# A hybrid decoder layer on one core: a second buffer for the prompt rows of the compression, value products given out later, and identity transposes at the start

## The chip, the cores and the metric

The kernel runs on one core of a Trainium2 chip. The metric is the device time of one execution in microseconds (us); lower is better. The core has TensorE (PE in the profile, with PEld for its weight loads), VectorE (DVE), ScalarE (ACT), GpSimd (POOL) and SyncE (SP). DMA transfers are issued from SP's and POOL's queues, each of which works in its own order: an issue that has to wait holds up all issues behind it on that queue.

## The reference, cut to what matters

One layer of a decoder trunk is computed for 512 prompt tokens and for 32 sample tokens (8 samples of 4), which share all weights; the model width is 2048 and everything is float32. After an RMSNorm one input projection (2048 by 7712) gives the queries, keys, values, gates and forget values of two groups of eight heads of 128:

```
z = einsum('btd,dc->btc', h, w_in)
out = einsum('bnchd,cde->bnhe', blk + pe, w)            # compress: 32 rows to one, for keys and for values
o = g[0] * o_compressed + g[1] * o_selected + g[2] * o_window      # the nsa group
s = q.k * scale + dq - dk ; o = softmax(s).v                       # the fox group, D = cumsum(log f)
y = x + einsum('btc,cd->btd', concat(o_n * silu(z_n), o_f * silu(z_f)), w_out)
```

For the samples the keys and values of 1024 earlier tokens lie in pages of 128 rows that a page table names, for both groups, and the nsa group has a window buffer of 512 rows besides. New keys and values go out as results; a final RMSNorm closes the trunk. The nsa group's compressed keys and values come from the cache's rows for the samples and from the new rows for the prompt.

## The kernel before, in words

**Tiles of the input projection.** The projection is cut into tiles of 128 output columns (`run_tiles`). A tile takes four loads of weights (`raw`, 256 KB each). `w_split` makes of each a high part on ACT (`whi`) and a low part on DVE (`wlo`), and PE adds the three products of high and low parts (`mm3`) in the PSUM tiles `pz`; so a quarter of a tile is 24 products of 128 by 272. Five `raw` buffers and three `whi`/`wlo` buffers let the loads and splits run ahead: the split is written two quarters before its products, and the load of a later quarter is written behind the `wlo` that frees its buffer. Quarters are numbered m; tile 0 (gates and forget values) has a path of its own in float32 (`w`), and the quarters 4, 5, ... belong to tiles 1, 2, .... Afterwards a tile's result `zt` goes to its `post` function, which for keys and values transposes it on DVE (`nat`) and writes it out (`store_natural`).

**What orders the work.** Everything else is written as Python generators, "streams": `start` (normalisation and transposition of x), `compress`, `nsa_prompt`, `nsa_sample`, `fox_sample`, `fox_prompt` and others. While the kernel is built, a model of the engines (`Clock`) keeps a time for each engine and for the DMA queues. Between products of the projection `S.pump()` lets each stream go on that is due by this clock. A stream that yields a list of tiles goes on once the model takes these tiles for ready; `S.after(us)` lets it go on once the model's PE is `us` further; a string waits for a flag. The result is a fixed order on each engine; on the chip only semaphores hold instructions back. So the pieces of the streams stand between the products of the projection, and a wrong guess of the model becomes a wait at the head of an engine's queue.

**The places of the change.** The compression's generator `compress` first takes the prompt's rows, which the tiles "c00 c01" (keys) and "c10 c11" (values) have just written to the result `nsa_kv_prompt`: for each of the two it waits for the flags, loads the rows back into the tile `cz` with eight DMAs of 16 by 8 by 128, yields `[cz]` and `S.after(8.0)`, and transposes them on DVE into `more0` or `more1`. There is one `cz` buffer, so the loads for the values wait for the transposition for the keys. Then 64 steps with gathered cache rows (`crow`, transposed into `ct`, split into `cxh`/`cxl`) and weights (`cw`) follow.

`fox_sample` is run twice, for four heads each. Its last part multiplies the probabilities `pt` (`fpt` in the profile) with pages of values `fpg`: two query groups `bq` of four steps `kp`, each with two pages of 256 KB. There are two page buffers, and the next two pages' loads are written behind the products (`ahead`), half of them on SP and half on POOL. The products go to the PSUM tile `accv`. `nsa_sample` has a similar end for each of two groups of samples: six steps of two sets of rows `spg` (five buffers), products in `acc`; the same five buffers carry the sets for its scores, which DVE transposes into `skt`.

`start` loads x in four quarters of 512 columns (`xt`, the first in two halves) and transposes each with 16 PE transposes (`pre`), from which ACT makes `h_hi` and DVE `h_lo`. Before x arrives it gives 16 transposes of the identity (`tr<-ident`) to PE, and 17 small ones of the norm's weights and of the samples.

Of the kernel before, what the change touches and what calls it, by code (L numbers as in the profile page):

```python
# [8 lines left out]
F32 = mybir.dt.float32  # L9
# [6 lines left out]
P = 128  # L16
# [283 lines left out]
def dram(ap, offset, dims):  # L300
    return bass.AP(tensor=ap.tensor, offset=ap.offset + offset, ap=dims)
# [3 lines left out]
def trunk_step(ctx, tc, x_prompt, x_sample, cache_nsa_kv, cache_fox_kv, cache_fox_logf, state_nsa_win,  # L305
# [4 lines left out]
    nc = Engines(tc.nc, clock)  # L310
# [20 lines left out]
    S = Streams(clock)  # L331
# [44 lines left out]
    def tr_tile(shape, name="tr"):  # L376
        return psum.tile(shape, F32, name=name, tag="tr", bufs=2)
# [4 lines left out]
    def cp(out, in_, scale=1.0):  # L382
        nc.scalar.activation(out, in_, AF.Copy, scale=scale)
# [19 lines left out]
    def mm(out, a, b, start=True, stop=True):  # L403
        nc.tensor.matmul(out, a, b, start=start, stop=stop, skip_group_check=True)
# [8 lines left out]
    ident = cst.tile([P, P], F32, name="ident")  # L413
# [457 lines left out]
    def load(t, src):  # L871
        nc.sync.dma_start(t, src)
        return t
# [210 lines left out]
    def fox_sample(hh):  # L1084
# [119 lines left out]
        for bq in range(2):  # L1204
            acc = psum.tile([P, SEQ], F32, name="accv", tag="accv", bufs=1)
            for kp in range(4):
                pgs = [pages.pop(at[1] + x) for x in range(2)]
                yield [*pgs, pt, acc]
                for x in range(2):
                    kb = kp * 2 + x  # L1210
                    for b in range(4):
                        o = kb * P + (bq * 4 + b) * 16
                        mm(acc[b * 32:b * 32 + 32], pt[:, o:o + 32], pgs[x][:, b], kb == 0, kb == 7)
                at[1] += 2
                yield
                ahead()
            ob = obs[bq]
            cp(ob, acc)
            yield
            yield from S.take()  # L1220
            tp = tr_tile([P, 4, P])
            for g in range(4):
                nc.tensor.transpose(tp[:, g, :], ob[:, g * P:(g + 1) * P], ident)
            yield
            for g in range(4):
                nc.vector.tensor_copy(o_s[:, 8 + hh * 4 + g, bq * 16:bq * 16 + 16].rearrange("p (b t) -> p b t", t=4),
                                      tp[:, g, :].rearrange("p (b r) -> p b r", r=32)[:, :, g * 4:g * 4 + 4])
            S.put()
# [17 lines left out]
    def compress(pl):  # L1246
# [17 lines left out]
        def load_w(s):  # L1264
            if s < 32:
                cg, kv, dp = s // 4, s // 2 % 2, s % 2
                cw[s] = t = pl.tile([P, 2, P], F32, name="cw", bufs=3)
                for d in range(2):
                    load(t[:, d], dram(cmp_w, (kv * 32 + cg * 4) * P * P + (dp * 2 + d) * 32 * P, [[P * P, 4], [P, 32], [1, P]]))
        load_rows(0)  # L1270
        load_w(0)
        load_w(1)
        more = []
        for kv in range(2):
            yield (f"nkv{kv}0", f"nkv{kv}1")
            yield [dram(nsa_kv_prompt, kv * 256 + v * P, [[1024, SEQ], [1, P]]) for v in range(2)]
            cz = pl.tile([P, 8, P], F32, name="cz")
            for c in range(4):
                for v in range(2):
                    load(cz[c * 32 + v * 16:c * 32 + v * 16 + 16],  # L1280
                         dram(nsa_kv_prompt, kv * 256 + v * P + c * 1024, [[32 * 1024, 16], [4 * 1024, 8], [1, P]]))
            yield [cz]
            yield S.after(8.0)
            m = pl.tile([P, 32, MORE], F32, name=f"more{kv}")
            more.append(m)
            nc.vector.memset(m[:, :, 33:], 0.0)
            nc.vector.tensor_copy(m.rearrange("p (g d) k -> p g d k", d=4)[:, :, :, 32],
                                  peT[:, :, kv * 8:kv * 8 + 8].rearrange("p d g -> p g d"))
            nc.vector.transpose(m[:, :, :32], cz.rearrange("p g d -> p (g d)"))
            yield  # L1290
# [12 lines left out]
        for step in steps + [None]:  # L1303
            if step:
                cg, bh, kv, dp = step
# [6 lines left out]
                n = 256 if bh else WIDE  # L1312
# [19 lines left out]
        for kv in range(2):  # L1332
            bc = pl.tile([P, 1], F32, name="bc", bufs=2)
            nc.vector.tensor_copy(bc, pss[kv][:, 288:289])
            pc = pl.tile([P, 32], F32, name="pc", bufs=2)
            nc.vector.tensor_scalar(pc, pss[kv][:, 256:288], bc, None, op0=OP.add)
            vt = pl.tile([P, 2, 8, 32], F32, name="vt", bufs=2)
            for bh in range(2):
                src = (psb[:, kv] if bh else pss[kv][:, :256]).rearrange("p (b v n) -> p v b n", b=4, v=2)
                for v in range(2):  # L1340
                    nc.scalar.activation(vt[:, v, bh * 4:bh * 4 + 4], src[:, v], AF.Identity, bias=bc)
            yield
            vf = vt.rearrange("p v b n -> p v (b n)")
            if kv == 0:
                nc.sync.dma_start(kp_scr, pc)
                nc.sync.dma_start(kc_scr, vf)
            else:
                yield from S.take(2)
                tp = tr_tile([P, 2, 256])
                for grp in range(2):  # L1350
                    for v in range(2):
                        nc.tensor.transpose(tp[:, grp, v * P:(v + 1) * P], vf[:, v, grp * P:(grp + 1) * P], ident)
                tq = tr_tile([16, 2, P])
                for v in range(2):
                    nc.tensor.transpose(tq[:, v, :], pc[:, v * 16:(v + 1) * 16], ident)
                yield
                vn = pl.tile([P, 2, 256], F32, name="crow", bufs=2)
                cp(vn, tp)
                vq = pl.tile([P, 2, P], F32, name="cw", bufs=3)[:16]
                cp(vq, tq)  # L1360
                S.put(2)
                yield
                nc.sync.dma_start(vc_scr, vn)
                nc.sync.dma_start(vp_scr, vq)
# [188 lines left out]
    def nsa_sample(pl):  # L1553
# [82 lines left out]
        for grp in range(2):  # L1636
# [14 lines left out]
            for x in range(2):  # L1651
                a, b = slice(64 * x, 64 * x + 64), slice(64 - 64 * x, 128 - 64 * x)
# [66 lines left out]
            for br in range(2):  # L1719
# [34 lines left out]
                p = T("sp", [P, 1024 + 64]) if br == 0 else p  # L1754
# [51 lines left out]
            def values(k, srcs, n=P, first=False, last=False):  # L1806
                for bb in range(4):
                    mm(acc[bb * 32:bb * 32 + 32], PT[:n, k, bb * 32:bb * 32 + 32], srcs[bb], first, last)
            yield [acc, PT]
            for k in range(0, 12, 2):  # L1810
                ts = [got.pop(0) for _ in range(2)]
                yield ts + [vc] * (k == 8)
                if k == 8:
                    values(12, [vs] * 4, 64)
                    values(13, [vc[:, grp, :]] * 4)
                for x in range(2):
                    values(k + x, [ts[x][:, bb] for bb in range(4)], first=k + x == 0, last=k + x == 11)
                yield ts
                set_in()
                set_in()  # L1820
# [82 lines left out]
    def add_in(col, post):  # L1903
# [4 lines left out]
                 n=lambda h, _: add_in(C_QN + h * P, post_qn(h)),  # L1908
                 q=lambda h, _: add_in(C_QF + h * P, post_qf(h)),
                 k=lambda h, _: add_in(C_KF + h * P, post_kf(h)),  # L1910
                 v=lambda h, _: add_in(C_VF + h * P, post_vf(h)),
# [6 lines left out]
    def start():  # L1918
        with tile_pool("pre") as pre:
# [27 lines left out]
            ts = tr_tile([P, KT, 32], "pres")  # L1947
            for k in range(KT):
                nc.tensor.transpose(ts[:, k, :], xs[:, k * P:(k + 1) * P], ident[:32, :32])
            for k in range(KT):  # L1950
                c = k // 4
                if k % 4 == 0:
                    yield [xt[:, c]]
                tag, bufs = (("s", 2), ("accv", 1), ("s", 2), ("acc", 1))[k % 4]
                tp = psum.tile([P, SEQ], F32, name="pre", tag=tag, bufs=bufs)
                yield [tp]
                for i in range(4):
                    nc.tensor.transpose(tp[:, i * P:(i + 1) * P], xt[:, c, i, (k % 4) * P:(k % 4 + 1) * P], ident)
                g = gT[:, k:k + 1]
                nc.scalar.activation(h_hi[:, k, :SEQ], tp, AF.Copy, scale=g)  # L1960
                nc.vector.scalar_tensor_tensor(h_lo[:, k, :SEQ], tp, g, h_hi[:, k, :SEQ], op0=OP.mult, op1=OP.subtract)
                flags.add(f"x{k}")
                if k == 3:
                    flags.add("begun")
                    hs = pre.tile([P, KT, 32], F32, name="hs")
                    nc.vector.tensor_tensor(hs, ts, gT[:, :, None].to_broadcast([P, KT, 32]), op=OP.mult)
                    cp(h_hi[:, :, SEQ:], hs)
                    low(h_hi[:, :, SEQ:], h_lo[:, :, SEQ:], hs)
# [186 lines left out]
```

## Time and profile before

| what | value |
|---|---|
| time, median of 3 runs | 1295.4 us (1294.78 to 1297.54) |
| time of the profiled execution | 1292.8 us, of which the span of the profile is 1291.1 us |
| PE busy | 1254.9 us, 97% of the span |
| DVE, ACT, POOL busy | 784.5, 549.8, 284.5 us |
| share of the chain that ended last | PE 73%, DMA 10%, "issue" 9% |
| input projection with all streams | from 16.8 to 1082.7 us |
| output projection | from 1082.7 us to the end |
| DMA | 266.86 MB, 207 GB/s in the mean |

The span is cut into slices on the profile's page, and a row of it shows the busy share of each engine. An engine's row in a timeline is its start, its duration, the engine, the operation with the tiles written and read, the number of merged instructions and, in square brackets, the idle time before it and what ended it. In the table of waits a row names who waited for whom, the sum in us, the number of times and the longest. A table of windows gives the busy time of each engine in a stretch, with the number of instructions in brackets, then the granted share of the PE clock, the DMA share and GB/s.

### The profile page before, as it was taken

How to read it: one execution, taken by the hardware profiler on the slowest of the kernel's cores; microseconds unless marked ns; L12 is line 12 of the kernel's file. 1: busy time of each engine (PE TensorE's matmuls, PEld its weight loads, DVE VectorE, ACT ScalarE, POOL GpSimd, SP SyncE). 2: the span in 40 equal slices, each digit the busy share in tenths (PEclk: the TensorE clock that was granted, in tenths of full speed). 3: DMA queues.
4: the chain of work that ended last, by engine and by line, in shares of the span. 5: the costliest groups of instructions: out<-in, count | busy, mean ns of one | idle time of the engine just before them, and what ended most of it. 6: DMA issues, size and time to landing. Idle time of an engine off the chain costs nothing.

```text
span 1291.1 us, 27195 instructions
## 1 busy us (share of the span) xinstructions
PE 1254.9 (97%) x10071; PEld 1130.4 (88%) x10071; DVE 784.5 (61%) x1978; ACT 549.8 (43%) x1193; POOL 284.5 (22%) x376
## 2 busy tenths in 40 slices
PE   8989999999999999999999999899999999999997
PEld 6989999998789999999998888688889988777786
DVE  6735888885546667655687753386566537354255
ACT  5313333434334677652345452256754524333221
POOL 5221277753410000005445012211111200000000
PEclk9989999999999999999999999999999999999999
DMA  7476699998986455659967688977788697334323
GB/s 214 129 192 170 178 279 298 299 288 272 295 272 160 121 157 155 174 157 292 294 199 235 174 239 244 257 211 198 217 233 202 196 304 258 100 114 147 127 76 139
DMA packets 308398, 266.86 MB, mean 207 GB/s; under 512 B 87198, under 2 KB 255150, under 8 KB 307592
## 3 DMA queue, kind: packets, MB, share of 16 engines
q1 hardware_dynamic: 284312, 189.15, 51.4%
q0 software_dynamic: 23904, 75.84, 18.3%
q8 instruction: 79, 1.29, 0.4%
q14 instruction: 55, 0.45, 0.1%
q10 hardware_dynamic: 48, 0.13, 0.0%
HBM read 236.32 MB, written 37.05 MB: 212 GB/s over the span
## 4 chain that ended last, share of the span: by engine, by line
PE 73%; DMA 10%; issue 9%; POOL 2%; DVE 2%; SPq 2%; ACT 2%; POOLq 0%; DVEq 0%; ACTq 0%
PE pz L169 40%; PE po L169 15%; DMA fpg<-in_cache_fox_kv 4%; PE tr L169 4%; PE accv L169 4%; PE s L169 4%; PE acc L169 3%; SPq L169 2%; DMA spg<-in_cache_nsa_kv 1%; POOL crow L169 1%; PE psb L169 1%; DMA spg<-in_state_nsa_win 1%; PE accf L169 1%; DMA xt<-in_x_prompt 1%; POOL fpg L169 1%
## 5 line engine op out<-in xcount | busy, mean ns | idle before, releaser
L169 PE MATMUL pz<-h_hi,whi 128*128 128x272 f32 x1920 | 565.6, 295 | 2.2 <-DVE zt L169 1.6
L169 PE MATMUL pz<-h_hi,wlo 128*128 128x272 f32 x1920 | 554.9, 289 | 5.8 <-DVE wlo L169 5.8
L169 PE MATMUL pz<-h_lo,whi 128*128 128x272 f32 x1920 | 554.4, 289 | 0.0
L169 PEld LDWEIGHTS pz<-h_hi,whi 128*128 128x128 f32 x1920 | 363.4, 189 | 18.2 <-issue 13.6
L169 PEld LDWEIGHTS pz<-h_hi,wlo 128*128 128x128 f32 x1920 | 362.8, 189 | 6.0 <-DVE wlo L169 6.0
L169 PEld LDWEIGHTS pz<-h_lo,whi 128*128 128x128 f32 x1920 | 363.3, 189 | 0.8
L169 DVE TENSOR_TENSOR wlo<-raw,whi 128x512 fp32r<-128x512 f32 x275 | 186.0, 678 | 157.7 <-ACT whi L169 152.9
L169 ACT ACTIVATE whi<-raw 128x512 fp32r<-128x512 f32 x275 | 171.5, 625 | 210.4 <-PE pz L169 96.9
L169 POOL DMA_INDIRECT fpg<-in_cache_fox_kv,fi x128 | 131.6, 1028 | 300.4 <-ACT whi L169 209.7
L169 PE MATMUL po<-whi,h_hi 128*128 128x512 f32 (+1 forms) x256 | 95.5, 373 | 0.0
L169 POOL DMA_INDIRECT crow<-in_cache_nsa_kv,ci x64 | 66.0, 1031 | 125.6 <-DVE ct L169 71.8
L169 PE MATMUL po<-whi,h_lo 128*128 128x512 f32 (+1 forms) x256 | 93.4, 365 | 0.0
L169 PE MATMUL po<-wlo,h_hi 128*128 128x512 f32 (+1 forms) x256 | 93.4, 365 | 0.0
L169 DVE STREAM_TRANSPOSE ft<-fpg 128x1024 f32<-128x1024 f32 x64 | 78.9, 1235 | 17.3 <-DMA fpg<-in_cache_fox_kv,fi 13.2
L169 ACT ACTIVATE cxh<-ct 128x580 fp32r<-128x580 f32 (+1 forms) x64 | 42.2, 660 | 85.1 <-DVE ct L169 75.2
L169 DVE TENSOR_TENSOR zt<-pz,rsb 128x272 f32<-128x272 f32 x56 | 24.6, 439 | 85.3 <-PE pz L169 85.3
L169 POOL DMA_DIRECT2D spg<-in_cache_nsa_kv x64 | 35.0, 546 | 185.3 <-DVE skt L169 57.6
L169 ACT ACTIVATE zt<-pz 128x272 f32<-128x272 f32 x66 | 26.2, 398 | 98.7 <-PE pz L169 98.5
L169 PEld LDWEIGHTS po<-whi,h_hi 128*128 128x128 f32 x256 | 48.1, 188 | 19.7 <-ACT whi L169 7.5
L169 POOL DMA_DIRECT2D fpg<-in_cache_fox_kv x64 | 34.8, 544 | 133.8 <-PE accv L169 96.0
L169 DVE TENSOR_TENSOR cxl<-ct,cxh 128x580 fp32r<-128x580 f32 (+1 forms) x64 | 46.1, 720 | 19.4 <-ACT cxh L169 18.6
L169 PEld LDWEIGHTS po<-whi,h_lo 128*128 128x128 f32 x256 | 48.2, 188 | 8.5
(409 smaller groups left out, 1907.1 us busy)
## 6 DMA issues: line engine op xcount, KB each, us to landing
raw<-in_w_in SPq DMA_DIRECT2D x240, 256.0 KB
fpg<-in_cache_fox_kv POOLq DMA_DIRECT2D x64, 256.0 KB, 7.0
fpg<-in_cache_fox_kv SPq DMA_DIRECT2D x64, 256.0 KB
raw<-in_w_out SPq DMA_DIRECT2D x40, 256.0 KB
spg<-in_cache_nsa_kv POOLq DMA_DIRECT2D x64, 128.0 KB, 5.4
spg<-in_cache_nsa_kv SPq DMA_DIRECT2D x64, 128.0 KB
out<-in_state_nsa_win SPq DMA_DIRECT2D x32, 254.0 KB
scr_z<-zt SPq DMA_DIRECT2D x28, 272.0 KB
```

What stands on the lines that cost most here:

```text
L169: return fn(*a, **k)
```

## The change

The change has four edits.

1. In `compress` the loads of the prompt's rows for the keys and for the values are written in a first loop, into two `cz` buffers, and both transpositions in a second loop behind it, each with its own `[cz]` and `S.after(8.0)`. The small tile `vt` at the end of `compress` becomes a part of a `cz` buffer, so that the memory stays the same.
2. In `fox_sample` every step of the value products waits a further `S.after(1.5)` once its pages are due.
3. In `nsa_sample` every step of the value products does the same.
4. In `start` a function `keep_on` gives 14 transposes of the identity to PE, into a PSUM tile that nobody reads. It is called before the first quarter's transposes and again behind them.

```diff
@@ fox_sample
             for kp in range(4):
                 pgs = [pages.pop(at[1] + x) for x in range(2)]
                 yield [*pgs, pt, acc]
+                yield S.after(1.5)
                 for x in range(2):
@@ compress
-        more = []
+        more, czs = [], []
         for kv in range(2):
             yield (f"nkv{kv}0", f"nkv{kv}1")
             yield [dram(nsa_kv_prompt, kv * 256 + v * P, [[1024, SEQ], [1, P]]) for v in range(2)]
-            cz = pl.tile([P, 8, P], F32, name="cz")
+            czs.append(pl.tile([P, 8, P], F32, name="cz", bufs=2))
             for c in range(4):
                 for v in range(2):
-                    load(cz[c * 32 + v * 16:c * 32 + v * 16 + 16],
+                    load(czs[kv][c * 32 + v * 16:c * 32 + v * 16 + 16],
                          dram(nsa_kv_prompt, kv * 256 + v * P + c * 1024, [[32 * 1024, 16], [4 * 1024, 8], [1, P]]))
+        for kv, cz in enumerate(czs):
             yield [cz]
             yield S.after(8.0)
             m = pl.tile([P, 32, MORE], F32, name=f"more{kv}")
...
-            vt = pl.tile([P, 2, 8, 32], F32, name="vt", bufs=2)
+            vt = pl.tile([P, 8, P], F32, name="cz", bufs=2)[:, :4].rearrange("p (v b) (c n) -> p v (b c) n", v=2, n=32)
@@ nsa_sample
                 ts = [got.pop(0) for _ in range(2)]
                 yield ts + [vc] * (k == 8)
+                yield S.after(1.5)
                 if k == 8:
@@ start
             for k in range(KT):
                 nc.tensor.transpose(ts[:, k, :], xs[:, k * P:(k + 1) * P], ident[:32, :32])
+            idle = tr_tile([P, 4, P])
+
+            def keep_on():
+                for k in range(14):
+                    nc.tensor.transpose(idle[:, k % 4, :], ident, ident)
+            keep_on()
             for k in range(KT):
...
                 if k == 3:
+                    keep_on()
                     flags.add("begun")
```

Since the planner's clock sees all four edits, it places the streams' pieces anew from there on. Three places show this. In what follows `-` is the kernel before and `+` the changed one.

PE's order at the start (`tr<-ident` are the identity's transposes, `pre` those of x, `pres` those of the samples):

```order
-L169 MATMUL pre<-ident,xt 128x128 x32
+L169 MATMUL tr<-ident 128x128 x14
+L169 MATMUL pre<-ident,xt 128x128 x16
+L169 MATMUL tr<-ident 128x128 x14
+L169 MATMUL pre<-ident,xt 128x128 x16
```

Fourteen transposes stand ahead of the first quarter of x, and fourteen between the first and the second.

DVE's order where the compression's prompt rows are transposed (`more`, from `cz`), between the splits of weights for m = 16, 17 and later:

```order
 L169 TENSOR_TENSOR wlo<-raw,whi 128x512
 L169 TENSOR_TENSOR zt<-pz,rsb 128x272
-L169 MEMSET more_993 128x32
-L169 COPY more_993<-peT 128x32
-L169 STREAM_TRANSPOSE more_993<-cz 128x32x32
-L169 TENSOR_TENSOR wlo<-raw,whi 128x512
-L169 TENSOR_TENSOR zt<-zt,rsb 128x272
+L169 TENSOR_TENSOR wlo<-raw,whi 128x512
+L169 TENSOR_TENSOR zt<-pz,rsb 128x272
 L169 STREAM_TRANSPOSE nat<-zt 128x544
 L169 TENSOR_TENSOR wlo<-raw,whi 128x512 x3
```

The first transposition no longer stands ahead of the split for m = 17; in the changed kernel it comes ten splits later, behind that for m = 26, and the second one three splits behind it.

SP's order behind the loads of `cz` and the writes `scr_f` of that time:

```order
 L169 DMA scr_f<-ft 4x32x128 x4
-L169 DMA raw<-in_w_in 128x4x128 x2
-L169 DMA out<-nat 4x32x32
-L169 DMA out<-nat 32x16x32 x4
+L169 DMA raw<-in_w_in 128x4x128
+L169 DMA out<-nat 4x32x32
+L169 DMA out<-nat 32x16x32 x2
+L169 DMA raw<-in_w_in 128x4x128
+L169 DMA out<-nat 32x16x32 x2
 L169 DMA raw<-in_w_in 128x4x128 x3
```

Three writes of results now stand ahead of the load of weights for m = 22.

## The prediction

> **What bounds the kernel now.** I read the page first, then PE's waits, then the windows around the longest of them.
>
> ```profile
> span 1291.1 us, 27195 instructions
> PE 1254.9 (97%) x10071; PEld 1130.4 (88%) x10071; DVE 784.5 (61%) x1978; ACT 549.8 (43%) x1193; POOL 284.5 (22%) x376
> ```
>
> PE is busy for 97% of the span and no other engine for more than 61%. So PE's order is the path: a microsecond counts if PE stands still in it or runs at less than its full clock, and 1291.1 − 1254.9 = 36 us is all the standing still there is. The table of PE's waits names most of it:
>
> ```profile
> PE pz L169 <- DVE wlo L169: 5.8, 1, 5.8
> PE accv L169 <- DMA fpg<-in_cache_fox_kv: 5.2, 6, 1.5
> PE pre L169 <- DMA xt<-in_x_prompt: 2.4, 2, 1.3
> PE acc L169 <- DMA spg<-in_state_nsa_win: 2.1, 1, 2.1
> PE pz L169 <- DVE zt L169: 1.6, 1, 1.6
> PE accf L169 <- DVE fptl L169: 1.6, 1, 1.6
> PE tr L169 <- DVE scr L169: 1.5, 1, 1.5
> ```
>
> The change aims at the first four rows, 15.5 us together. The rest are single short waits that a new order may lengthen or shorten.
>
> **Edit 1, the compression's prompt rows.** The timelines of DVE and PE show where the 5.8 us come from:
>
> ```profile
> 79.68 1.25 DVE L169 STREAM_TRANSPOSE more<-cz 128x1024 f32<-128x1024 f32 x1 [8.10 <-DMA cz<-out]
> 80.85 0.65 DVE L169 TENSOR_TENSOR wlo<-raw,whi 128x512 fp32r<-128x512 f32 x1
> 81.55 0.60 PE L169 MATMUL pz<-h_hi,wlo 128*128 128x272 f32 x1 [5.80 <-DVE wlo L169]
> ```
>
> DVE waits 8.1 us at the head of its queue for the rows in `cz`; behind it stands the low part of the weights of m = 17, and PE waits for that. In the changed order this split comes first and the transposition ten splits later. At the pace of the splits (ACT rows below, one each 3.0 us) that is 30 us, and 8.1 are needed, so the wait goes whole: −5.8. After the wait PE is slow for a while:
>
> ```profile
> 81.50:85.20 3.70, 3.65 (x16) 3.65 (x17) 2.27 (x4) 0.00 (x0) 0.00 (x0) 0.51 0.83 270
> 85.20:92.00 6.80, 6.80 (x56) 6.80 (x56) 1.73 (x3) 1.27 (x2) 0.00 (x0) 1.00 0.74 174
> ```
>
> At a granted clock of 0.51 sixteen products take 3.7 us; at 1.00 56 take 6.8, 0.121 each, and sixteen 1.9. Without the standstill this stretch has its clock, −1.8. What is late next is the supply of weights, for SP is full just then:
>
> ```profile
> 68.82 5.75 SPq L169 DMA_DIRECT2D cz<-out  x8
> 74.67 0.53 SPq L169 DMA_DIRECT2D raw<-in_w_in  x1
> 75.71 3.57 SPq L169 DMA_DIRECT2D scr_f<-ft  x4
> 79.38 2.52 SPq L169 DMA_DIRECT2D raw<-in_w_in  x2
> 82.66 4.18 SPq L169 DMA_DIRECT2D out<-nat  x5
> ...
> 89.12 0.63 ACT L169 ACTIVATE whi<-raw 128x512 fp32r<-128x512 f32 x1 [2.38 <-PE pz L169]
> 92.13 0.63 ACT L169 ACTIVATE whi<-raw 128x512 fp32r<-128x512 f32 x1 [2.37 <-PE pz L169]
> ...
> 872.83 5.21 DMA raw<-in_w_in
> ```
>
> The load at 74.67 is that of m = 20; those of 21 and 22 follow at 79.38. In the changed order three of the five `nat` writes (0.84 us each by the row) get ahead of m = 22, so it goes out at about 79.4 + 1.3 + 2.5 = 83.2. With 5.2 us for a load (the last row, from the chain of waits) it lands at 88.4, and `whi` and `wlo` (0.63 and 0.65) make it ready at about 89.8. PE stops at 81.55 − 5.80 = 75.75, a few products into m = 17, which began at 75.4; no longer held, it would begin m = 22 five quarters of 3.0 us later, at 90.4. That is cover by 0.6 us only. For m = 21 (out at 79.4, ready at 86.0, due at 87.4) it is 1.4. If a load took 7.6 us, as the page load at 820.51 below, m = 22 would be 1.8 late; I take 0.4 between 0 and 1.8. The compression itself begins later, by two waits of 8 us on the planned clock instead of one after the second load; products of the projection fill that. Edit 1: −5.8 − 1.8 + 0.4 = −7.2, bounds −7.6 and −5.8.
>
> **Edits 2 and 3, the value products.** The 5.2 us of the second wait fall into the two runs of `fox_sample` (the same table, cut at 296 to 385 and at 740 to 832 us):
>
> ```profile
> PE accv L169 <- DMA fpg<-in_cache_fox_kv: 2.3, 3, 0.8
> PE accv L169 <- DMA fpg<-in_cache_fox_kv: 2.9, 3, 1.5
> ```
>
> None is over 1.5 us, so products that stand 1.5 us further back find their pages, if the pages come when they come now. They don't quite: the next pages are loaded into the buffers that these products free, so each load moves as well, by 1.5 us for each step before it; but the interval between one step's products and the next step's grows by the same 1.5, and the wait is set by this interval alone. In the chain of waits the steps and loads read so:
>
> ```profile
> 763.84 1.85 PE accv L169 x16
> 774.32 1.85 PE accv L169 x16
> ...
> 800.66 9.94 DMA fpg<-in_cache_fox_kv
> ...
> 820.51 7.61 DMA fpg<-in_cache_fox_kv
> ```
>
> Steps are 10.5 us apart and a load takes up to 9.9 after its issue. For the first run I take −2.1 of 2.3. In the second run the changed order puts more of the samples' sets `spg` among the pages: on POOL's queue 14 set loads stand among the last 16 page loads, where there were two. So I take −1.0 of 2.9. The single wait in `nsa_sample` was 2.1 us; 1.5 of it is covered, −1.5. It too is followed by a stretch at half clock:
>
> ```profile
> 945.30:948.70 3.40, 1.32 (x14) 0.64 (x13) 1.17 (x4) 2.45 (x5) 2.20 (x4) 1.00 1.13 279
> 948.70:952.20 3.50, 3.45 (x20) 2.64 (x20) 0.43 (x2) 1.21 (x4) 0.71 (x2) 0.51 1.09 266
> ```
>
> At 0.51 instead of 1.00 3.5 us hold 1.7 of loss. Whether the clock falls depends on how idle PE is in the 3.4 us before (1.32 busy here), so I count −1.2. The delays lengthen the streams by 16 × 1.5 = 24 us (fox) and 12 × 1.5 = 18 us (nsa), which costs only what the projection can't cover; the chain has this cover:
>
> ```profile
> 1051.11 31.57 PE pz L169 x252
> ```
>
> After the last step of `nsa_sample` 31.6 us of products of the projection remain, and in the changed order there are more of them behind it (339 products of `pz` behind the last `acc`, 261 before, counted in the two orders). Cost 0; without that cover it would be up to 18. Edits 2 and 3: −2.1 − 1.0 − 1.5 − 1.2 = −5.8; bounds 0 and −(5.2 + 2.1 + 1.7) = −9.0.
>
> **Edit 4, the transposes at the start.**
>
> ```profile
> 1.52 3.68 PE L169 MATMUL tr<-ident 128*128 128x128 f32 x16 [1.52 <-DVE ident L169]
> 5.26 1.91 PE L169 MATMUL pres<-ident,xs 32*128 32x32 f32 x16
> 8.43 3.70 PE L169 MATMUL pre<-ident,xt 128*128 128x128 f32 x16 [1.26 <-DMA xt<-in_x_prompt]
> 13.23 3.65 PE L169 MATMUL pre<-ident,xt 128*128 128x128 f32 x16 [1.10 <-DMA xt<-in_x_prompt]
> ...
> 16.88 2.45 PE pz L169 x40
> 19.34 1.94 PE pre L169 x16
> ...
> 12.81 1.77 SPq L169 DMA_DIRECT2D xt<-in_x_prompt  x2
> ```
>
> Sixteen transposes take 3.7 us at 8.43 and at 13.23 and 1.94 at 19.34: PE begins at half pace and is at full pace after 16.9. The table of windows gives 1.00 for this stretch; here the durations tell more. Fourteen more at half pace are 14 × 0.23 = 3.2 us in gaps of 1.26 and 1.10, so the first quarter's transposes begin at 7.2 + 3.2 = 10.4 instead of 8.43. The pace doubled after 3.65 us of transposes without a gap; from 7.2 on PE would have no gap. If full pace comes at 10.4, all 60 transposes end at 10.4 + 46 × 0.121 = 16.0, if it comes at 14, at 7.2 + 6.8 + 30 × 0.121 = 17.6; now it is 16.88. The gain ends at the third quarter of x, issued at 12.81 (1 MB; the second quarter's took until 13.09, when the rows of `pre` follow it): the 40 products of tile 0 fill the time up to 19.34 with it. I take 0; the bounds are −0.9 and, if full pace doesn't come at all before the first products, +5.5 (below).
>
> **The sum.** −7.2 − 5.8 + 0 = −13.0 against the profiled execution of 1292.8: 1279.8. This execution is 2.6 us under the median of the runs, 1295.4 (1294.78 to 1297.54), so the forecast for the median is 1282.4, a ratio of 0.990. What the new order does to the other short waits (the last three rows of the waits are 4.7 us) I take as 0 ± 3.
>
> **The rivals.**
> - *The value products gain nothing* (edits 2 and 3 at their bound 0): the page loads move with the products, and what made them late, other traffic, is there again. For it: the 9.94 us load against steps 10.5 apart. Against: no wait was over 2.1. 1282.4 + 5.8 = 1288.2.
> - *Another wait takes the place of the one at 75.8*: a head of DVE's queue that waits for rows, or weights that come late between 80 and 95 us. For it: SP's full queue above. Against: later the splits run well ahead, as ACT's rows with PE as their releaser show. It costs what edit 1 brings: 1282.4 + 7.2 = 1289.6.
> - *The identity's transposes don't raise the clock.* They then add 2 × 3.2 − 1.26 − 1.10 = 4.1 us, and the products of tile 0 run at half pace until they have worked for as long as the transposes of the second quarter did, 3.65 us, a loss of 1.8; less the 0.4 that PE waits for the third quarter: +5.5, 1287.9. Against: the pace doubled at 16.9 after nothing but transposes. The Trainium skill's page "TensorE: Matmul & The Clock Gate", Part 4, says that transposes don't count as a busy PE for the clock; by it edit 4 would cost these 5.5 us. The trace disagrees: 3.65 us of transposes at 13.23 were followed by a full clock.
> - *Both of the first two*: nothing is gained, 1282.4 + 13.0 = 1295.4.
> - *Slower: pages queue behind the samples' sets.* On POOL the second run's last page loads now stand behind sets 6 and 7, and there are five set buffers, so these wait until DVE has transposed sets 1 and 2 for the scores. What such a wait has cost POOL (its waits from 800 to 1040 us):
>
> ```profile
> POOL spg L169 <- DVE skt L169: 57.6, 9, 25.7
> ```
>
>   Products due 10.5 + 1.5 = 12 us after the pages' buffers are free, loads of 7.6: a wait W at the head makes PE late by W + 7.6 − 12. With the longest, 25.7, that is 21.3, with 1.7 for half a clock afterwards 23.0: 1305.4. The whole is slower than before by more than 2.6 us from W − 4.4 + 1.7 = 13.0 + 2.6 on, W = 18.3. Against: the longest waits belong to later sets, when nothing else was due; the two here wait for the first transpositions.
>
> **How the numbers follow.** Chances: forecast 0.52 (its own range 1278 to 1287: ± 3 for the order and ± 1.5 for the terms), the value products gain nothing 0.17, another wait 0.12, no clock 0.06, nothing gained 0.08, slower 0.05. About 0.2%, 2.6 us, is what a measurement of this kernel can tell from no change; so faster means below 1292.8 and slower above 1298.0. The first four cases are faster, 0.87 together; I give 0.85, since another wait can be larger than the one removed. Same is 0.10, slower 0.05. The range 1277 to 1292 leaves out some 0.06 below and 0.14 above.
>
> **What would show it.** Right: no PE wait for `wlo` near 75 us and no stretch at 0.51 behind it; DVE's transposition of `cz` without idle time before it; `accv <- DMA fpg` under 2 us in the sum over both runs; the third quarter's `pre` within 0.5 us of 19.3. Wrong: a PE wait for `whi` or `wlo` between 80 and 95 (the supply of weights), waits of `accv` as long as now, `pre` of the second quarter ending after 18 us, or a POOL wait for `skt` with `fpg` loads behind it.

## The result and the profile after

The changed kernel takes 1301.28 us (median of 20 runs, 1295.05 to 1307.79); the kernel before, run beside it, takes 1295.76 (20 runs, 1289.30 to 1298.78). The ratio is 1.0052, 95% interval 1.0038 to 1.0066. So the change makes the kernel 5.5 us slower where 13 us less were forecast, and the time lies outside the range 1277 to 1292. The profiled execution took 1300.94 us.

The head of the page of the changed kernel:

```profile
span 1299.1 us, 27235 instructions
...
PE 1255.2 (97%) x10099; PEld 1131.0 (87%) x10099; DVE 785.4 (60%) x1978; ACT 547.5 (42%) x1187; POOL 285.9 (22%) x376
```

PE is busy as long as before (1254.9), so in the sum the 8.0 us of longer span are standing still: 1299.1 − 1255.2 = 43.9 us, where it was 36.2. The busy time also holds the stretches in which PE ran at half its clock, those that have gone and those that have come, so the standing still is not the whole of the loss. PE's waits in the changed kernel (who waited for whom, us in total, times, longest):

```profile
PE pz L169 <- DVE zt L169: 9.4, 3, 5.7
PE tr L169 <- DMA fqb<-out: 4.9, 1, 4.9
PE s L169 <- DMA kvc<-scr_kc: 4.5, 1, 4.5
...
PE accv L169 <- DMA fpg<-in_cache_fox_kv: 0.7, 2, 0.4
```

Three of the four rows that the change aimed at have gone or shrunk: the wait for `wlo` of 5.8 us (three short ones elsewhere, 1.7 together, are left), the one of `acc` for the set `spg` (no row left), and `accv` waits 0.7 us for pages where it was 5.2. The fourth, `pre` waiting for x, has grown from 2.4 to 3.7. Three single waits that the kernel before did not have have come: 4.5 us for the compressed keys `kvc` at 818.85, 5.7 us for `zt` at 850.19, 4.9 us for the own values `fqb` at 867.07. All three lie in one stretch, and each leads into a stretch at half clock (table of windows: behind the stretch its length and PE's busy time, at the end the granted clock, the DMA share and GB/s):

```profile
820.83:827.66 6.83, 4.35 (x16) 1.77 (x20) 1.47 (x5) 1.12 (x3) 0.01 (x1) 0.50 0.94 271
...
854.97:861.79 6.82, 5.88 (x26) 2.68 (x26) 2.99 (x5) 1.12 (x2) 1.11 (x2) 0.50 0.93 200
...
872.03:878.88 6.85, 6.85 (x31) 6.79 (x32) 0.29 (x1) 0.66 (x2) 0.00 (x0) 0.50 0.49 145
```

PE is busy for 4.35 + 5.88 + 6.85 = 17.1 us in them; if that work takes half as long at the full clock, they cost some 8.5 us (an estimate) beside the 15.1 us of waits: about 24 us in 60. The kernel before had waits of its own in these stages, so the net loss is smaller: where the two orders agree on PE, the changed kernel is 4.1 us ahead at 162 us and 8.1 us behind at 1059 us, 12.2 us lost in between.

The orders on PE tell what stands there. Before the change the first product of `nsa_sample` followed directly on the last one of `fox_sample`:

```
L169 MATMUL tr<-fpn,fqb 128x32 x4
L169 MATMUL tr<-gat_s,sel 128x24
```

In the changed kernel `tr<-gat_s,sel` stands 192 products of the projection ahead of `tr<-fpn,fqb`, and three of the eight value steps of `fox_sample` come behind it. Two sample stages, which both live on loads from the cache, now run at the same time: on SP and on POOL alike 14 loads of sets stand ahead of the last page load, where there were two. SP's timeline shows what this does (the start, the time that the issues took, the queue's operation, the number of issues):

```profile
811.10 3.79 SPq L169 DMA_DIRECT2D vs<-out  x4
815.49 2.40 SPq L169 DMA_DIRECT2D fpg<-in_cache_fox_kv  x4
817.94 0.42 SPq L169 DMA_DIRECT2D kvc<-scr_kc  x1
...
853.54 6.61 SPq L169 DMA_DIRECT2D spg<-in_state_nsa_win  x8
...
860.97 1.75 SPq L169 DMA_DIRECT2D spg<-in_state_nsa_win  x4
...
863.66 3.32 SPq L169 DMA_DIRECT2D spg<-in_state_nsa_win  x4
867.08 0.38 SPq L169 DMA_DIRECT2D scr_m<-zt  x1
867.50 0.43 SPq L169 DMA_DIRECT2D fqb<-out  x1
```

The chain of waits has what they then take to land:

```profile
817.94 5.32 DMA kvc<-scr_kc
...
867.50 4.36 DMA fqb<-out
```

The load of `kvc` goes out 0.9 us before PE stops for it, and that of `fqb` 0.4 us after PE has stopped. Both stand on SP right behind loads of the other stage, `kvc` (256 KB) behind pages and `fqb` (64 KB) behind sets. The third wait comes by way of DVE:

```profile
845.30 1.25 DVE L169 STREAM_TRANSPOSE skt<-spg 128x1024 f32<-128x1024 f32 x1 [6.48 <-DMA spg<-in_cache_nsa_kv]
...
851.41 1.25 DVE L169 STREAM_TRANSPOSE skt<-spg 128x1024 f32<-128x1024 f32 x1 [4.29 <-DMA spg<-in_cache_nsa_kv]
...
855.34 0.43 DVE L169 TENSOR_TENSOR zt<-pz,rsb 128x272 f32<-128x272 f32 x1
```

DVE stands at the head of its queue for sets of rows that have not landed; the copy `zt` behind them, which frees a PSUM tile for the projection, comes late, and PE waits.

### The profile page after: what moved, and what is told of

The parts are those of the page before. It is cut to its first block, busy times and chain, and to the rows that moved or that the text cites. A ratio compares the mean times of both kernels' runs of the same rounds, so it can differ in the third digit from the quotient of the medians.

```text
span 1299.1 us, 27235 instructions
## 1 busy us (share of the span) xinstructions
PE 1255.2 (97%) x10099; PEld 1131.0 (87%) x10099; DVE 785.4 (60%) x1978; ACT 547.5 (42%) x1187; POOL 285.9 (22%) x376
## 4 chain that ended last, share of the span: by engine, by line
PE 80%; DMA 11%; SPq 3%; DVE 3%; ACT 2%; issue 1%; DVEq 0%; ACTq 0%
PE pz L169 45%; PE po L169 15%; PE s L169 5%; PE tr L169 5%; PE accv L169 4%; DMA raw<-in_w_in 4%; PE acc L169 3%; SPq L169 3%; PE psb L169 2%; DMA spg<-in_cache_nsa_kv 2%; DMA spg<-in_state_nsa_win 1%; PE accf L169 1%; DMA i<-scr_c 1%; DMA dsb<-scr_d 1%; DMA xt<-in_x_prompt 1%
## 5 line engine op out<-in xcount | busy, mean ns | idle before, releaser
L169 DVE TENSOR_TENSOR zt<-pz,rsb 128x272 f32<-128x272 f32 x62 | 27.2, 438 | 77.3 <-PE pz L169 77.1
L169 DVE TENSOR_TENSOR cxl<-ct,cxh 128x580 fp32r<-128x580 f32 (+1 forms) x64 | 46.1, 721 | 16.0 <-ACT cxh L169 14.4
```

What stands on the lines that cost most here:

```text
L169: return fn(*a, **k)
```

## The experiments

Theory **overlap**: the loss comes from the two sample stages running into each other, which edits 1 and 2 each bring about through the planner's clock; the edits themselves do what the forecast says. Rival **delay**: the delayed value products lengthen the stages and cost it. Rival **transposes**: the work added at the start costs it. The fourteen runs went to chips of two kinds: on one kind the kernel before takes 1295 us, on the other 1356 to 1361. A time is therefore compared only with times of the same chip, and across chips only ratios are.

**Each edit alone.** The four kernels hold edit 1, 2, 3 or 4 of the diff and nothing else. In their orders on PE, edit 1 alone and edit 2 alone bring the overlap (two and three value steps of `fox_sample` behind the first product of `nsa_sample`); edit 3 and edit 4 alone do not.

> Edit 1 alone (two buffers for the prompt rows). In its order nsa_sample starts among fox_sample's last three steps of value products, as in the changed kernel; before, it starts behind them. Theory 'overlap' (the loss comes from the two stages' loads sharing SP's queue, and any edit that lets them overlap has it): a gain of some 3.4 us near 80 us, and waits of PE of 10 to 24 us with half clock between 780 and 880 us, so 1300 to 1315. Theory 'delay' (the value products' delay in fox_sample is what costs): 1292, with no such waits. Theory 'transposes' (the identity transposes cost): 1292.

> Edit 2 alone (1.5 us of planned delay for the value products of fox_sample). Its order overlaps the two stages as well. Overlap: the waits on accv shrink from 5.2 to under 1.5 us, the waits of the overlap come, 1303 to 1318, and the 5.8 us for wlo near 76 us stay. Delay: the same direction, 1301 to 1306. Transposes: 1293.

> Edit 3 alone (the same delay in nsa_sample). The order of all that comes before nsa_sample's value products is that of before, with no overlap. Overlap and delay: 1292 to 1296, the wait of 2.1 us on acc gone or under 0.7. Transposes: 1296.

> Edit 4 alone (28 identity transposes). The order on the engines is that of before but for them. Overlap and delay: no change, 1295 to 1297, third quarter's transposes within 0.5 us of 19.3. Transposes: 1299 to 1302, the third quarter's transposes begin 3 us later or more.

Measured, with the kernel before at 1360.77:

| edit | median us | ratio | 95% interval |
|---|---|---|---|
| 1, rows | 1369.31 | 1.0072 | 1.0047 to 1.0098 |
| 2, fox delay | 1369.87 | 1.0095 | 1.0064 to 1.0126 |
| 3, nsa delay | 1355.74 | 0.9982 | 0.9954 to 1.0009 |
| 4, transposes | 1359.43 | 0.9984 | 0.9958 to 1.0010 |

The two edits with the overlap cost 9 us each, the two without it cost nothing. "Transposes" falls, and "delay" cannot explain edit 1, which delays no value product. The signs named beforehand came for edit 3 (no wait of `acc` for sets) and edit 4 (the third quarter's transposes begin at 19.3 us). For edit 2 one did not: PE's waits for pages were to fall under 1.5 us and are 5.4, all of them between 840 and 960 us, where the stages meet. Which loads come late differs from order to order. In that stretch PE waits with edit 1 alone 3.7 us for `skt`, 3.5 for pages, 3.3 for `kvc` and 3.1 for `sp`; with edit 2 alone 7.5 for `fqb`, 5.4 for pages and 3.1 for `sp`.

**A gate on the overlap.** All four edits stay; `nsa_sample` starts behind a flag that `fox_sample` sets after the seventh of eight value steps of its second run. In the order `tr<-gat_s,sel` then stands where `fox_sample` ends. The changed kernel ran beside it on the same chip.

```diff
@@ fox_sample, behind a step's products
+                if hh and bq * 4 + kp == 6:
+                    flags.add("late")
                 at[1] += 2
@@ nsa_sample
-            f"nkv{s}{v}" for s in range(2, 6) for v in range(2))
+            f"nkv{s}{v}" for s in range(2, 6) for v in range(2)) + ("late",)
```

> The changed kernel itself, as the measure for the three versions below on the same chip. Both theories: 1.005 times the time before, with its three waits of 4 to 6 us between 815 and 880 us (for the compressed keys kvc, for zt behind skt, for fqb).

> All four edits stay; nsa_sample may begin only when seven of the eight value steps of the second run of fox_sample are done (a flag set there). In the order, its first product then stands at the end of fox_sample again, as before the change, and its last one 230 products of the projection later than in the changed kernel. Theory 'overlap' (the loss comes from the loads of two sample stages on SP and POOL at once): the waits for kvc, for zt behind skt and for fqb go, 15 us, and the half clock behind them, some 8; the two stages keep some 6 us of small waits: 18 us less than the changed kernel, in a range of 12 to 24, so 0.991 times the time before (0.987 to 0.996). Rival 'delay' (the delayed value products themselves lengthen the stage): as the changed kernel, 1.005. Rival 'tail': nsa_sample now ends so late (108 products of the projection remain, 13 us) that PE waits at its end for what the overlap cost before: 0.998 to 1.006, with waits for sp, tr or acc after 1050 us.

Measured: the kernel before 1294.95, the changed one 1301.62 (ratio 1.0051, 1.0032 to 1.0070), the gated one 1284.31 (0.9926, 0.9900 to 0.9951), 17.3 us less than the changed kernel where 18 were expected. PE's waits from 780 to 900 us, the longest of the changed kernel here, then all of the gated one:

```profile
PE tr L169 <- DMA fqb<-out: 6.5, 1, 6.5
PE pz L169 <- DVE zt L169: 5.1, 1, 5.1
PE s L169 <- DMA kvc<-scr_kc: 2.4, 1, 2.4
```

```profile
PE tr L169 <- DVE scr L169: 4.2, 1, 4.2
PE accv L169 <- DMA fpg<-in_cache_fox_kv: 2.2, 3, 1.6
PE tr L169 <- DMA fqb<-out: 1.7, 1, 1.7
PE s L169 <- DMA kvc<-scr_kc: 0.2, 1, 0.2
```

The three waits fall from 14.0 to 1.9 us; two others, for `scr` and for pages, take 6.4 us there. "Tail" does not show: PE has no wait behind 1050 us. This is the main finding, and it holds without the edits being taken out: the loss is the overlap.

**Edits 1 and 2 alone, with the gate.**

> The first edit alone (two buffers for the prompt's rows), with the gate on nsa_sample, so without the overlap. The forecast had -7.2 us for this edit. With the weights of m = 21 late, as the changed kernel shows (1.6 to 2.5 us, 1.7 of half clock): -3 to -5, so 0.997 (0.995 to 0.998); if the forecast's term holds, 0.994; if the gain is taken up by the new order elsewhere, 1.000 and above.

> The delay of the value products in fox_sample alone, with the gate on nsa_sample, so without the overlap. Forecast's term: -3.1 us, 0.9976. Rival, from the two gated versions with and without it (1282.0 and 1279.0): it costs 3 us, 1.002.

Measured, with the kernel before at 1361.42: edit 1 with the gate gives 1352.67, ratio 0.9933 (0.9910 to 0.9956), where it was 1.0072 without the gate; edit 2 gives 1356.35, ratio 0.9953 (0.9928 to 0.9977), where it was 1.0095. For each the gate is worth 1.4%. The intervals hold what the forecast gave them (7.2 us, 0.56%, and 3.1 us, 0.24%) as soon as the two stages stand apart. The gate was not put into the kernel before alone, so whether it brings something by itself is open; there, as in the gated versions, two loads of sets stand ahead of the last page load on each queue.

**Edits 3 and 4 together.**

> Edits three and four alone (value products of nsa_sample later, transposes at the start); in the order the two sample stages don't overlap. Forecast's terms: -1.5 - 1.2 + 0 = -2.7 us, 0.998, with the wait of acc for spg gone. Rival (nothing gained, as the two apart left open): 1.000.

Measured 1357.58, ratio 0.9962 (0.9942 to 0.9981); the wait of `acc` for `spg` is gone. The forecast's terms (0.998) lie in the interval.

**What in the overlap costs it: two loads.** The overlap stays, and so does the order of PE up to it; of PE's 10099 instructions about 500 stand elsewhere, most of them behind 950 us. In the source only the load of `kvc` for the first group is written at the head of `nsa_sample`, and that of `fqb` behind the fifth value step instead of the eighth.

```diff
@@ fox_sample, ahead of a value step (the same lines behind the steps: only for hh = 0)
+                if hh and bq and kp == 1:
+                    yield tuple(f"v{4 * hh + g}" for g in range(4))
+                    vsn = fx.tile([P, 4, 4, 64], F32, name="fqb")...
+                    load(vsn, dram(fox_kv_sample, 1024 + hh * 512, [[2048, 32], [1, 512]]))
@@ nsa_sample
+        kc0 = load(T("kvc", [P, 2, 256]), kc_scr)
         yield [qz, r, sm, jz, sel_v]
...
-            kc = load(T("kvc", [P, 2, 256]), kc_scr)
+            kc = load(T("kvc", [P, 2, 256]), kc_scr) if grp else kc0
```

> All four edits and the overlap of the two sample stages stay (the order of PE is that of the changed kernel but for a few rows); only two loads are issued sooner on SP: the compressed keys kvc ahead of the samples' sets instead of behind six of them and twelve page loads, the own values (fqb) after the fifth value step of fox_sample instead of after the eighth, ahead of the eight loads of the window's set. Theory 'head of SP's queue' (the loads were issued late because SP stood behind loads whose buffers were not free): the waits for kvc and fqb go, 8.9 us in the changed kernel on the last chip, and one of the two long half-clock stretches, 3.4: 12 us less than the changed kernel (8 to 14), 0.996 times the time before, while the wait of 5 us for zt behind skt stays. Rival 'traffic' (two stages' loads at once take that long wherever they are issued): the waits move to the next loads, 1.002 to 1.006.

Measured 1364.29 against 1361.42, ratio 1.0000 (0.9976 to 1.0025), between the two expectations. The waits for `kvc` and `fqb` were gone, but the changed kernel had not run on that chip, so nothing followed on what the two loads are worth. Then both ran side by side:

> The changed kernel beside the version with two early loads, on one chip. Both theories: 1.005 times the time before where the time before is 1295, and 1.005 to 1.012 where it is 1361, as the single edits were there (1.007 and 1.010).

> The version with only kvc and fqb loaded sooner, on the same chip as the changed kernel. Theory 'head of SP's queue': 8 to 14 us less than the changed kernel in this call, with no wait of PE for kvc or fqb; what remains against the gated version is the wait for zt behind skt and its half clock, 5 + 3. Rival 'traffic': within 3 us of the changed kernel.

Measured, with the kernel before at 1355.92: the changed kernel 1364.23, ratio 1.0076 (1.0050 to 1.0102), the one with two early loads 1351.79, ratio 0.9983 (0.9951 to 1.0014): 12.4 us less, where 12 were expected (8 to 14). PE's waits from 850 to 960 us, the changed kernel and then the one with early loads:

```profile
PE tr L169 <- DMA fqb<-out: 6.9, 1, 6.9
PE pz L169 <- DVE zt L169: 5.3, 1, 5.3
PE s L169 <- DMA kvc<-scr_kc: 3.7, 1, 3.7
```

```profile
PE s L169 <- DVE skt L169: 5.0, 2, 2.7
PE pz L169 <- DVE zt L169: 3.6, 1, 3.6
```

SP's timeline for `kvc` in these two kernels, in the same order:

```profile
881.07 0.42 SPq L169 DMA_DIRECT2D kvc<-scr_kc  x1
```

```profile
851.39 0.36 SPq L169 DMA_DIRECT2D kvc<-scr_kc  x1
```

The load goes out 30 us sooner, and the wait is gone although the same bytes are moved in the same stretch. The two executions are level up to there (the 4250th product of the projection begins at 842.4 and 842.5 us) and 14.4 us apart at the last product (1157.4 and 1143.0). So it is the place in SP's queue, not the traffic of two stages as such, that makes these two waits; "traffic" falls for them. The waits behind `skt` are 8.6 us instead of 5.3: how much of those is the queue's order and how much the transfers was not taken apart. Nor did the gated version run on this chip, so what is left of the overlap's cost with the two loads early has no number.

**The wait at 86.8 us.** In the changed kernel PE waits 2.5 us there for `zt`. SP's timeline and DVE's:

```profile
74.81 1.68 SPq L169 DMA_DIRECT2D raw<-in_w_in  x1
77.01 3.44 SPq L169 DMA_DIRECT2D scr_f<-ft  x4
80.56 1.24 SPq L169 DMA_DIRECT2D raw<-in_w_in  x1
81.90 3.91 SPq L169 DMA_DIRECT2D out<-nat  x3
```

```profile
88.19 0.69 DVE L169 TENSOR_TENSOR wlo<-raw,whi 128x512 fp32r<-128x512 f32 x1 [3.88 <-ACT whi L169]
88.80 0.43 DVE L169 TENSOR_TENSOR zt<-pz,rsb 128x272 f32<-128x272 f32 x1
```

The load at 80.56 is that of m = 21, 1.2 us later than before, and it took 6.9 us to land by the chain of waits; its low part is split at 88.19, for which DVE has stood 3.9 us at the head of its queue. The copy `zt` behind it frees the PSUM tile that PE needs in the middle of m = 20. In the next kernel the first load of the prompt's rows (`cz`, eight issues at 68.67, 6 us of SP) is written beside the second one, behind the values' flags:

```diff
@@ compress
-            yield (f"nkv{kv}0", f"nkv{kv}1")
+            yield ("nkv00", "nkv01", "nkv10", "nkv11")
```

> As the gated version, and the first of the two loads of the prompt's rows (eight DMAs, 6 us of SP at 68 us) is issued behind the values too, beside the second. Theory 'supply' (the wait for weights at 86.8 us comes from SP being full between 68 and 88 us, the prompt's rows among it): the load of the weights of m = 21 goes out before 78 instead of 80.6, PE's wait of 2.5 us and the 1.7 us of half clock behind it go: 4 us less than the gated version (2.5 to 4.5), so 0.988 where that is 0.991. Rival 'moved': the sixteen DMAs of both loads now stand together and hold weights back there by 6 us more; the wait is at 90 to 105 us instead: the gated version's time.

Measured, on the chip of the gated version, 1282.05, ratio 0.9889 (0.9864 to 0.9915), 2.3 us under the gated version, just short of the range of "supply" (2.5 to 4.5); the two intervals overlap, so the time alone does not settle it. SP issues m = 21 sooner, and there is no wait of PE between 74 and 100 us; the gated version has one of 1.8 there:

```profile
74.11 0.44 SPq L169 DMA_DIRECT2D raw<-in_w_in  x1
```

**Without the delay in `fox_sample`.** The same kernel with edit 2 taken out, gate and late rows kept:

> As the one before, without the delay of the value products in fox_sample. Theory of the forecast (this delay brings 3 us of the waits for fpg): 3 us slower than the version before it (1 to 5), with waits for fpg of some 5 us in the table. Rival (the delay moves the loads with the products and gains nothing, or costs what it lengthens): the same within 1.5 us, or faster.

Measured 1278.99 (1278.31 to 1280.10), ratio 0.9871 (0.9846 to 0.9896): 3.1 us faster than with the delay (1280.32 to 1283.58), not 3 us slower. It is the fastest of all, 16 us under the kernel before, and beats both kernels. The 3 us do not arise where the two stages meet. Aligned on the places where their orders agree, the profiled execution without the delay is 0.5 us behind at 288 us, 3.5 ahead at 385 us, and 3.5 ahead at the end. PE's waits from 300 to 400 us, in the first run of `fox_sample`, with the delay and then without it:

```profile
PE pz L169 <- DVE zt L169: 2.2, 1, 2.2
PE accv L169 <- DMA fpg<-in_cache_fox_kv: 0.5, 1, 0.5
```

```profile
PE pz L169 <- DVE zt L169: 0.5, 1, 0.5
PE accv L169 <- DMA fpg<-in_cache_fox_kv: 0.5, 1, 0.5
```

With the delay PE waits 1.7 us longer for the copy `zt`, and a stretch at a granted clock of 0.50 follows (359.85 to 363.26 us, 1.7 us by the same estimate); without it there is none. From 780 to 920 us the waits balance: the delay saves 1.1 us of those for pages (1.9 against 3.0), and all waits together are 9.6 and 9.5 us. Alone, with the gate, on the other kind of chip, the delay gained 0.5%. Its sign depends on the order around it; why `zt` comes late in this order was not settled.

## Why the prediction was wrong

The step that failed stands at the end of the sum: "What the new order does to the other short waits (the last three rows of the waits are 4.7 us) I take as 0 ± 3." It took the waits of the old trace as all that a new order can move. What moved was larger than a wait, namely the start of a stage, and it brought 15.1 us of new waits and 8.5 us of half clock. With the gate the same four edits give a ratio of 0.9926, 10.6 us less than the kernel before (1294.95 − 1284.31); the forecast was 0.990, 13.0 us. So the sum of the edits' own terms came near, and the one term at "0 ± 3" was some 17 us off (1301.62 − 1284.31). That the sum came near is in part luck, for the single terms don't bear it out: edit 1 was mis-sized, and edit 2 changes its sign with the order. On the slower chips the parts (0.9933 and 0.9953 with the gate, 0.9962 for edits 3 and 4) multiply to 0.985, more than the four together gave on the other.

Point by point:

- **Edit 1, the wait at 75.8.** Right: no wait of PE before 86.8, no idle time of DVE for `cz`. The term for the weights was mis-sized: 0.4 us, with "1.4" of cover for m = 21; measured in the profiled execution 2.5 us of wait through m = 21 and a stretch of 3.4 us at 0.50 behind it, some 1.7. The issue of the load of m = 20 took 1.68 us instead of 0.53, so the writes `scr_f` and then m = 21 went out 1.2 later; the load took 6.9 us where 5.2 were reckoned; and the cover was reckoned for the products of m = 21, while the copy `zt`, which stands behind that split on DVE, is needed earlier. The net gain in the profiled execution is 5.8 + 1.8 − 2.5 − 1.7 = 3.4 instead of 7.2. The second profiled execution of the changed kernel on a chip of this kind has 1.6 us of wait there and no half clock behind it, and edit 1 alone with the gate gained 0.67% on a slower chip; the three sizes were not reconciled.
- **Edit 2, `fox_sample`.** The waits for pages went further down than forecast, by 4.5 instead of 3.1 in this order; in the gated orders the delay itself is worth 1.0 of them (2.4 against 3.4 us over both runs), and in that pair of kernels it brings a wait for `zt` in the first run. That the longer stream "costs only what the projection can't cover" was wrong in kind: it did not cost at the end, it changed which stages lie beside each other.
- **Edit 3, `nsa_sample`.** Right on this chip: the wait for `spg` is gone and no cost shows. In the changed kernel on the slower chip a wait of 2.0 us for the same set is there.
- **Edit 4, the transposes.** Right in sum, third quarter included; the mechanism was the one described in some starts only. PE's timeline of the changed kernel:

```profile
1.52 3.67 PE L169 MATMUL tr<-ident 128*128 128x128 f32 x16 [1.52 <-DVE ident L169]
...
6.35 1.75 PE L169 MATMUL tr<-ident 128*128 128x128 f32 x14
...
19.27 1.94 PE L169 MATMUL pre<-ident,xt 128*128 128x128 f32 x16 [1.36 <-DMA xt<-in_x_prompt]
```

  The added transposes already run at the full pace (1.75 for 14), so they did not bring it; the 16 at 1.52, which the kernel before has too, did. The rule of the Trainium skill, "TensorE: Matmul & The Clock Gate", Part 4, that transposes don't count as a busy PE, is again contradicted by the trace: nothing but transposes had run.
- **The rivals.** The slower one named the right pair, the samples' sets and the pages on one queue, but the wrong queue and the wrong victim. It looked at POOL and at the pages; PE waits 0.7 us for pages. It was SP's queue, and what came late were two single loads that had no row in the old table, and sets on SP. It was given 0.05 although the sign was counted there, on POOL, where the same fourteen loads of sets stand ahead of the last page load.
- **What would show it** asked for a wait for `wlo` or `whi` between 80 and 95. It came, by way of `zt`, but is the small part of the miss. Nothing on the list concerned the stretch where the stages met.

## What to carry to other kernels

When an edit goes through a planner, first compare the two orders for where each stage begins and ends, and price every pair of stages that newly overlap: on an in-order queue, look for the single loads that are issued just before they are used; here two of them came late. A wait that the old trace shows as zero is not a bound on what it can become. A dependency written out between two stages can decide whether the tuning inside them pays: here it turned 6.7 us of loss into 10.6 us of gain.

## What the runs showed of the hardware

**The clock at the start depends on where a window falls.** In PE's timeline the full pace came after 16.9 us in the kernel before, at about 5 in the changed kernel, and at about 10.5 in the kernel without edit 2 (its rows of the added transposes below), though all three run the same instructions up to 6.3 us. (The table of windows gives 1.00 even at half pace there, so the pace is read from the durations.)

```profile
7.10 3.25 PE L169 MATMUL tr<-ident 128*128 128x128 f32 x14
...
12.07 1.69 PE L169 MATMUL tr<-ident 128*128 128x128 f32 x14
```

In this start the added transposes run at half pace at first, close the gap ahead of the first quarter, and bring the full pace before 16.9, as forecast; the end of the third quarter's load takes the gain away, as in the others. The granted clock changes at moments that are whole multiples of 3.413 us apart (above at 820.83, 827.66, 854.97 and 861.79: 2, 8 and 2 of them). In the changed kernel a window of that length held only 128-wide transposes (1.64 to 5.05); in the other two a window busy throughout but with 32-wide ones in it (3.24 to 6.66, 3.68 to 7.09) was not followed by the full pace. Of the sixteen profiled starts twelve reach the full pace between 4.4 and 5.8 us, with or without edit 4; three without it do so at 16.7 to 16.9, one with it at 10.5. That 32-wide transposes don't count is a guess from these and wasn't tested. The three early starts without edit 4 fall back to a granted clock of 0.50 for one window, between 8.1 and 12.5 us; none of the ten starts with edit 4 does. So the added transposes hold the clock through the gaps, though nothing comes of it ahead of the third quarter. The Trainium skill, "TensorE: Matmul & The Clock Gate", Part 1, calls the window free-running; the starts agree.

**How much standing still halves the clock.** Three windows of the gated version (PE's busy time is the second figure after the stretch):

```profile
86.70:90.11 3.41, 1.76 (x14) 1.77 (x15) 2.48 (x4) 1.15 (x2) 0.00 (x0) 1.00 1.07 248
356.36:359.77 3.41, 1.28 (x11) 1.08 (x10) 3.00 (x6) 1.49 (x4) 0.00 (x0) 1.00 0.88 280
861.53:864.94 3.41, 0.69 (x6) 0.72 (x7) 2.77 (x9) 2.31 (x5) 0.00 (x0) 1.00 0.30 76
```

After the first the clock stayed full; after the second and the third it was half for 3.4 us. The place of a wait decides as well as its length. The wait of 2.46 us at 86.83 in the changed kernel fell almost wholly into one window (PE busy 1.09 of 3.41 us from 86.97 on), and half clock followed. A wait of the same 2.46 us at 886.42 in the kernel without edit 2 was shared by two windows (busy 2.10 and 2.27), and the clock stayed full.

**Two kinds of chip.** The kernel before takes 1295 us on one kind and 1356 to 1361 on the other. On the slower kind PE stands still for causes that the profile does not name; the changed kernel's waits there have these rows first:

```profile
PE accv L169 <- issue: 13.4, 20, 1.3
PE pz L169 <- issue: 9.2, 19, 1.0
```

They lie between 75 and 330 and between 640 and 790 us, and short stretches of half clock follow them. What PE lacks there wasn't found. The ratios are therefore compared across the two with care. The changed kernel is the only one that ran on both, and its ratios are 1.005 and 1.008.
